# Split weight operands moved to 17 start offsets within larger buffers

## The chip, the cores and the metric

The kernel runs on one core of one Trainium2 chip. The metric is the device time of one execution in microseconds (us); the median of several runs is compared. The engines are called as in the profile: PE is TensorE's matmul stream, PEld its weight loads, DVE is VectorE, ACT is ScalarE, POOL is GpSimd, SP is SyncE, which here only issues DMAs.

## The reference, cut to what matters

One decoder layer over a sequence of 1024 rows of 1024 values, all in float32, and a last normalization:

```python
h = rms_norm(x, norm_mix)
proj = h @ w_in                       # 1024 x 8192, in eight groups of 1024 columns
xa, ga, q, f, v, g, m_a, m_b = split(proj)
y_a = rg_lru(conv(xa), w_r, w_i, ...) * gelu(ga)      # two 256-wide block products
y_b = rms_norm(hgrn2(silu(q), f, v)) * silu(g)
x = x + (sigmoid(m_a) * y_a + sigmoid(m_b) * y_b) @ w_out
h = rms_norm(x, norm_mlp)
x = x + square(relu(h @ w_up)) @ w_down               # 1024 x 4096, 4096 x 1024
return rms_norm(x, norm_final)
```

## The kernel before, in words

Every large product is made from three matmuls. `split` turns a float32 tile into a high part of type fp32r (ACT, line 76) and a low part, the difference (DVE, line 77). `mm3` (lines 113 to 117) adds high times low, high times high and low times high into one PSUM bank. In the trace a matmul reads `out<-moving,stationary`: `pj_f<-hT0H,wL` streams `hT0H` past the weights `wL`. The moving operand is 512 columns wide except in `project_v`, where it is 256.

The mixer takes the sequence in two halves (c = 0, 1) and each half in four pairs of heads (p = 0 to 3). For a pair, `project_v` makes v with the weights moving (out `pv`). `project` makes the other seven groups with the weights stationary and `hT`, the transposed input, moving (out `pj_xa`, `pj_q` and so on); `rg_lru` does its block products with the weights stationary and `xc` moving (out `pr`, `pi`). After four pairs `out_proj`, for c = 1 a loop of its own, multiplies by w_out with the weights moving (out `po`). The MLP works on 16 quads of hidden columns by a seven-product scheme: `hidden` streams `h2...` past split weights (out `uX`, `uY`, `uZ`), and the down products stream split weights past `u...` (out `dX`, `dY`, `dZ`), for two quads in turn, three matmuls for one quad and three for the other.

The numbered weight tiles are `wts[i]`, i from 0 to 75: 17 for a pair (v 0 and 1, xa 2 and 3, q 4 and 5, f 6 and 7, rg 8, then two each for g, mb, ga, ma), and eight of w_out. SP loads them into four buffers `raw`, and `split_w` (lines 87 to 92) splits each into `wH` and `wL`, which lie in six buffers under the tag `w`. The MLP's split tiles of 1024 columns lie in the same six buffers (line 771) for every quad up, and for one of the two quads of a down step. Buffers are taken as they come free; `split_w` has a raised priority, and its two instructions are kept in the order of the program up to the end of the first norm. A tile scheduler then orders the instructions of each engine by priority and writes the waits.

Byte addresses within a partition, as the allocator lays the buffers out: the six `w` buffers start at 23,296 and then every 4,096 bytes, `hT` fills 80,640 to 113,408, the split `xc` starts at 170,688, the `h2` tiles fill 114,624 to 229,312. In the down products the first quad's operands lie in the `w` buffers, in 47,872 to 56,064 and in 56,064 to 84,736, the second quad's at 131,008 to 163,776 (weights) and from 180,160 up (`u`). All of these starts are multiples of 64 bytes. Those of the `w` buffers, of `hT` and of the first quad are multiples of 256; those of `xc`, `h2` and of the second quad are 192 past a multiple of 256, so 64 past a multiple of 128. What a matmul reads starts at a multiple of 512 bytes within its tile.

Of the kernel before, what the change touches and what calls it, by code (L numbers as in the profile page):

```python
# [11 lines left out]
F32R = mybir.dt.float32r  # L12
# [6 lines left out]
P = 128  # L19
# [12 lines left out]
OUT_TILES = 8  # L32
QUADS = 16
LEVELS = (2, 8)


PV_LB, PV_CB, PV_BR, PV_BI, PV_LAM, PV_CW, PV_HG = 0, 8, 16, 24, 32, 40, 72
# [4 lines left out]
def trunk(ctx: ExitStack, tc: tile.TileContext, x, wts, mlp, pv, gains, mask_f, mask_u, out):  # L42
# [4 lines left out]
    wp = ctx.enter_context(tc.tile_pool(name="wp", bufs=1))  # L47
# [27 lines left out]
    def split(src, h, lo):  # L75
        keep(A.copy(h, src))  # L76
        keep(V.tensor_tensor(out=lo, in0=src, in1=h.bitcast(F32), op=ALU.subtract))  # L77
# [7 lines left out]
        return raw  # L85

    def split_w(i, raw):
        h = wp.tile([P, 1024], F32R, tag="w", name=f"wH{i}", bufs=6)
        lo = wp.tile([P, 1024], F32R, tag="w", name=f"wL{i}", bufs=6)
        with tc.high_priority(400):  # L90
            split(raw, h, lo)
        return h, lo
# [3 lines left out]
    def fill_w(n):  # L96
        while made[0] < min(n, len(seq)):
            i = seq[made[0]]
            raw = raws.pop(0) if raws else load_w(i)
            ready[made[0]] = split_w(i, raw)  # L100
            made[0] += 1
# [168 lines left out]
    def project(c, name):  # L270

        pp = [bank("pj", f"pj_{name}_{s}") for s in range(2)]
        for half in range(2):
            wh, wl = next_w()
            for k in range(4):
                hh, hl = kt(hT[c], 4 * half + k)
                for s in range(2):
                    cols = slice(k * 256 + s * P, k * 256 + (s + 1) * P)
                    mm3(pp[s], wh[:, cols], wl[:, cols], hh, hl, half == 0 and k == 0, half == 1 and k == 3)
        return pp  # L280
# [45 lines left out]
    def rg_lru(c, p, xc, xh, xl):  # L326
        wh, wl = next_w()
        hs = mt("h", f"h{c}{p}", (P, 2, T))
        for s in range(2):
            u = 2 * p + s  # L330
            pr, pi = bank("pj", f"pr{c}{u}"), bank("pj", f"pi{c}{u}")
            for o, k0 in ((pr, 0), (pi, 2)):
                for k in range(2):
                    cols = slice((k0 + k) * 256 + s * P, (k0 + k) * 256 + (s + 1) * P)
                    mm3(o, wh[:, cols], wl[:, cols], xh[:, k, :], xl[:, k, :], k == 0, k == 1)
            w = mt("rw", f"rw{c}{u}")
            A.activation(w, pr, AF.Sigmoid, bias=pvt[:, PV_BR + u : PV_BR + u + 1])
            A.activation(w, w, AF.Tanh, scale=sp4[:, u : u + 1])
            ig = mt("ri", f"ri{c}{u}")
            A.activation(ig, pi, AF.Sigmoid, bias=pvt[:, PV_BI + u : PV_BI + u + 1])  # L340

            V.tensor_scalar(w, w, 0.0, None, op0=ALU.max)
            rec = mt("rr", f"rr{c}{u}")
            V.tensor_scalar(rec, w, 1.0, None, op0=ALU.add)
            V.reciprocal(rec, rec)  # L345
            A.activation(w, w, AF.Sqrt)
            V.tensor_tensor(out=ig, in0=ig, in1=xc[:, s, :], op=ALU.mult)
            V.scalar_tensor_tensor(w, w, 2.0, rec, op0=ALU.mult, op1=ALU.mult)
            V.tensor_tensor(out=ig, in0=ig, in1=w, op=ALU.mult)
            V.tensor_scalar(rec, rec, 2.0, -1.0, op0=ALU.mult, op1=ALU.add)  # L350
            h = hs[:, s, :]
            V.tensor_tensor_scan(h, rec, ig, hcar[:, u : u + 1], op0=ALU.mult, op1=ALU.add)
            if c + 1 < NC:
                G.tensor_copy(hcar[:, u : u + 1], h[:, T - 1 : T])
        return hs
# [12 lines left out]
    def f_of(c, p, pp):  # L368
        ff = mt("f", f"f{c}{p}", (P, 2 * T))
        kk = mt("kk", f"kk{c}{p}", (P, 2 * T))  # L370
        for s in range(2):
            u = 2 * p + s
            f, k = ff[:, s * T : (s + 1) * T], kk[:, s * T : (s + 1) * T]
            A.activation(f, pp[s], AF.Sigmoid)
            A.activation(k, pp[s], AF.Sigmoid, scale=-1.0)
            V.tensor_scalar(f, f, omlb[:, u : u + 1], lb[:, u : u + 1], op0=ALU.mult, op1=ALU.add)
            V.tensor_scalar(k, k, omlb[:, u : u + 1], None, op0=ALU.mult)
        V.tensor_scalar(ff, ff, F_MIN, 1.0, op0=ALU.max, op1=ALU.min)
        return ff, kk

    def hgrn(c, p, q1, f, kk, v):
# [42 lines left out]

        for li, cw in enumerate(LEVELS):
            g = 256 // cw
# [199 lines left out]
    for c in range(NC):  # L626
# [6 lines left out]
        for p in range(NPAIR):  # L633
# [7 lines left out]
            f, kk = f_of(c, p, project(c, f"f{c}{p}"))  # L641
            with tc.high_priority(300):
                h = rg_lru(c, p, *xc3)
# [366 lines left out]
def _masks():  # L1010
# [3 lines left out]
    mu[:, 0, 0, :] = (t % 2 == 1) & (s == t - 1)  # L1014
    for i, c in enumerate(LEVELS):
        for d in (1, 2, 3):
# [32 lines left out]
```

## Time and profile before

| | before |
|---|---|
| median of 3 runs | 1634.1 us (1632.56 to 1635.3) |
| span of the profiled execution | 1630.3 us |
| PE busy | 1585.8 us, 97% |
| DVE busy | 1211.9 us, 74% |
| ACT busy | 762.2 us, 47% |
| PE matmuls, weight loads | 9240, 9240 |

The span runs from the first to the last instruction of the one execution that was profiled, and for that execution the page gives no other time; the median of the runs is 3.8 us above it. A record's duration of a matmul covers its whole way through the array, so consecutive records overlap. What a matmul costs in a dense stretch is read from the distance between the starts of consecutive ones.

### The profile page before, as it was taken

The numbers are of one execution on the slowest core, as the hardware profiler recorded it, in microseconds if no ns is written. First come the engines' busy times: TensorE is split into PE (matmuls) and PEld (weight loads), VectorE is DVE, ScalarE is ACT, GpSimd is POOL, SyncE is SP. The second block draws the span as 40 slices with busy tenths as digits, with TensorE's granted clock in tenths as the row PEclk, the third lists the DMA queues.
The fourth block names the chain that finished last, engine by engine and source line by source line (L and its number), as shares of the span: only waits on it lengthen the run. The fifth ranks groups of instructions, "written<-read, shape, count | busy, mean of one in ns | idle before, by whom it ended". The sixth has DMA issues, their size and how long they took to land.

```text
span 1630.3 us, 23190 instructions
## 1 busy us (share of the span) xinstructions
PE 1585.8 (97%) x9240; PEld 1303.6 (80%) x9240; DVE 1211.9 (74%) x1751; ACT 762.2 (47%) x1186; POOL 62.8 (4%) x99
## 2 busy tenths in 40 slices
PE   7999999999999999999999998999999999999998
PEld 6788788788788788788787876888888878888886
DVE  5975956848764965848759688977777888888876
ACT  4643545435442544436435566767766732221113
POOL 0010100100100000000100000000000000000000
PEclk9999999999999999999999998999999999999999
DMA  6222223223244222222222352666666566666652
GB/s 236 91 66 91 91 66 103 66 91 93 78 165 142 80 77 91 78 84 98 66 91 91 125 200 102 262 247 239 233 248 247 216 259 237 238 246 249 252 207 104
DMA packets 57996, 246.51 MB, mean 151 GB/s; under 512 B 6688, under 2 KB 6816, under 8 KB 47136
## 3 DMA queue, kind: packets, MB, share of 16 engines
q1 hardware_dynamic: 56304, 239.27, 40.8%
q10 hardware_dynamic: 1584, 5.77, 1.0%
q8 instruction: 72, 1.18, 0.3%
q14 instruction: 36, 0.29, 0.1%
HBM read 185.24 MB, written 59.77 MB: 150 GB/s over the span
## 4 chain that ended last, share of the span: by engine, by line
PE 82%; DVE 15%; issue 1%; ACT 1%; DMA 1%; POOL 0%; DVEq 0%; POOLq 0%; SPq 0%; ACTq 0%
PE dX L115 4%; PE dX L117 4%; PE dX L116 4%; PE uX L115 3%; PE uX L117 3%; PE uX L116 3%; DVE wL L77 2%; PE pj_ga L117 2%; PE pj_ga L116 2%; PE pj_ga L115 2%; PE pj_ma L117 2%; PE pv L116 2%; PE pv L115 2%; PE pj_ma L116 2%; PE pv L117 2%; PE pj_f L117 2%
## 5 line engine op out<-in xcount | busy, mean ns | idle before, releaser
L77 DVE TENSOR_TENSOR wL<-raw,wH 128x1024 fp32r<-128x1024 f32 x160 | 194.4, 1215 | 151.3 <-ACT wH L76 148.7
L76 ACT CAST wH<-raw 128x1024 fp32r<-128x1024 f32 x160 | 167.9, 1050 | 166.9 <-issue 67.1
L963 DVE TENSOR_TENSOR acc<-acc,dX 128x512 f32<-128x512 f32 x128 | 86.7, 682 | 29.6 <-PE dX L117 28.9
L76 ACT CAST wA<-q 128x512 fp32r<-128x512 f32 x32 | 19.8, 621 | 130.9 <-PE dX L117 82.8
L963 DVE TENSOR_TENSOR acc<-acc,dY 128x512 f32<-128x512 f32 x64 | 43.6, 683 | 16.6 <-PE dY L117 14.9
L345 DVE RECIPROCAL rr<-rr 128x512 f32<-128x512 f32 x16 | 53.5, 3345 | 0.0
L823 ACT ACTIVATE b<-b 128x512 f32<-128x512 f32 x48 | 30.2, 631 | 38.7 <-DVE b L822 38.6
L115 PE MATMUL pv<-wL,hT0H 128*128 128x256 f32 x128 | 37.1, 289 | 0.0
L117 PE MATMUL pv<-wH,hT0L 128*128 128x256 f32 x128 | 36.7, 286 | 0.0
L116 PE MATMUL pv<-wH,hT0H 128*128 128x256 f32 x128 | 36.6, 286 | 0.0
L115 PE MATMUL pv<-wL,hT1H 128*128 128x256 f32 x128 | 36.5, 285 | 0.0
L116 PE MATMUL pv<-wH,hT1H 128*128 128x256 f32 x128 | 36.2, 283 | 0.0
L117 PE MATMUL pv<-wH,hT1L 128*128 128x256 f32 x128 | 36.2, 283 | 0.0
L311 DVE SCALAR_TENSOR_TENSOR xc<-xp,pvt,xc 128x512 f32<-128x512 f32 x48 | 33.1, 746 | 0.0
L551 ACT ACTIVATE on<-po 128x128 f32<-128x128 f32 x64 | 17.0, 278 | 33.5 <-PE po L541 33.2
L570 ACT ACTIVATE smb<-pj_mb 128x512 f32<-128x512 f32 x16 | 9.6, 597 | 45.4 <-PE pj_mb L117 45.2
L824 ACT ACTIVATE b<-b 128x512 f32<-128x512 f32 x48 | 30.0, 629 | 1.1
L384 DVE TENSOR_TENSOR seg<-seg 128x128 f32<-128x128 f32 (+2 forms) x96 | 26.8, 309 | 0.2
L565 ACT ACTIVATE g<-pj_g 128x512 f32<-128x512 f32 x16 | 9.6, 598 | 37.2 <-PE pj_g L117 37.2
L444 POOL TENSOR_SCALAR seg<-seg 128x128 f32<-128x128 f32 (+1 forms) x16 | 12.6, 790 | 360.9 <-DVE seg L384 360.9
L117 PE MATMUL pj_ga<-hT1H,wL 128*128 128x512 f32 x64 | 26.5, 414 | 0.0
L115 PE MATMUL uX<-h2B11L,wA 128*128 128x512 f32 x64 | 26.2, 409 | 0.3 <-DVE rstd_h L137 0.3
(1854 smaller groups left out, 5258.3 us busy)
## 6 DMA issues: line engine op xcount, KB each, us to landing
raw<-wts_in SPq DMA_DIRECT2D x160, 512.0 KB, 3.5
q<-mlp_in SPq DMA_DIRECT2D x64, 512.0 KB, 4.0
x<-x_in SPq DMA_DIRECT2D x8, 512.0 KB, 5.6
acc<-x ACTq DMA_DIRECT2D x8, 512.0 KB, 6.0
y_out<-acc SPq DMA_DIRECT2D x16, 256.0 KB, 2.1
xs<-x_in SPq DMA_DIRECT2D x8, 256.0 KB, 4.2
x<-xs SPq DMA_DIRECT2D x8, 256.0 KB, 2.1
x2s<-x_in SPq DMA_DIRECT2D x4, 512.0 KB, 4.8
```

Source lines behind the costliest of these rows:

```text
L76: keep(A.copy(h, src))
L77: keep(V.tensor_tensor(out=lo, in0=src, in1=h.bitcast(F32), op=ALU.subtract))
L115: PE.matmul(o, ah, bl, start=first, stop=False, **how)
L116: PE.matmul(o, ah, bh, start=False, stop=False, **how)
L117: PE.matmul(o, al, bh, start=False, stop=last, **how)
L311: V.scalar_tensor_tensor(xc[:, s, :], xp[:, j : j + T], pvt[:, PV_CW + 8 * j + u : PV_CW + 8 * j + u + 1], xc[:, s, :], op0=ALU.mult, op1= ...
L345: V.reciprocal(rec, rec)
L384: mul = lambda o, a, b: V.tensor_tensor(out=o, in0=a, in1=b, op=ALU.mult)
L551: A.activation(on[:, 4 * s + n, :], po[:, n * P : (n + 1) * P], AF.Square, accum_out=ssq[:, 4 * s + n : 4 * s + n + 1])
L823: A.activation(b[:, at, :], b[:, at, :], AF.Relu, scale=-1.0 if at == 2 else 1.0)
L824: A.activation(b[:, at, :], b[:, at, :], AF.Square)
L963: V.tensor_tensor(out=dst, in0=dst, in1=banks[bk, pr], op=op)
```

## The change

A split weight tile no longer starts at the start of its buffer. The buffers of tag `w` grow from 1024 to 1072 elements of 4 bytes (4,288 bytes), and `wH` and `wL` of weight tile i are the 1024 elements that begin at element `START[i // 2 % 17]`: 0 to 48 elements, which is 0 to 192 bytes. High and low part of one tile have the same offset, and so have mostly the two tiles of a group.

```diff
+START = (0, 1, 2, 4, 6, 8, 10, 12, 14, 16, 24, 32, 36, 40, 44, 47, 48)
...
     def split_w(i, raw):
-        h = wp.tile([P, 1024], F32R, tag="w", name=f"wH{i}", bufs=6)
-        lo = wp.tile([P, 1024], F32R, tag="w", name=f"wL{i}", bufs=6)
+        at = START[i // 2 % len(START)]
+        h = wp.tile([P, 1072], F32R, tag="w", name=f"wH{i}", bufs=6)[:, at : at + 1024]
+        lo = wp.tile([P, 1072], F32R, tag="w", name=f"wL{i}", bufs=6)[:, at : at + 1024]
         with tc.high_priority(400):
             split(raw, h, lo)
```

The MLP's tiles under the same tag keep 1024 elements and start at the start of their buffer. But the buffers now stand 4,288 bytes apart, so every other one starts 64 past a multiple of 128. All that is allocated from the left behind them moves up by 6 x 192 = 1,152 bytes, which is nine times 128 and not a multiple of 256: `hT`, `xc` and the first quad's other tiles among them. What is allocated from the right (`h2`, the second quad's tiles) stays.

## The prediction

> **What bounds the kernel now.** I read the page first: busy times, slices, then the chain of work that ended last.
>
> ```profile
> PE 1585.8 (97%) x9240; PEld 1303.6 (80%) x9240; DVE 1211.9 (74%) x1751; ACT 762.2 (47%) x1186; POOL 62.8 (4%) x99
> ...
> PE   7999999999999999999999998999999999999998
> ...
> PEclk9999999999999999999999998999999999999999
> ...
> PE 82%; DVE 15%; issue 1%; ACT 1%; DMA 1%; POOL 0%; DVEq 0%; POOLq 0%; SPq 0%; ACTq 0%
> ```
>
> PE is busy in nearly every slice at the full granted clock, and the chain is PE for 82%. The table by stage says the same; its columns are the stretch in us, its length, then busy us of PE, PEld, DVE, ACT, POOL with instructions.
>
> ```profile
> 20.00:473.00 453.00, 446.08 (x3117) 373.26 (x3116) 322.02 (x503) 211.62 (x346) 31.87 (x47) 1.00 0.28 90
> ...
> 500.00:927.00 427.00, 421.46 (x2993) 351.92 (x2992) 295.06 (x437) 196.28 (x325) 20.78 (x28) 1.00 0.27 86
> ...
> 990.00:1314.00 324.00, 320.85 (x1369) 256.22 (x1367) 264.67 (x332) 224.01 (x320) 0.00 (x0) 1.00 0.60 228
> 1314.00:1620.00 306.00, 305.66 (x1319) 247.46 (x1320) 244.48 (x360) 65.02 (x92) 0.00 (x0) 1.00 0.58 224
> ```
>
> In the four dense stages, 1,510 us together, PE idles 16 us. So the change counts where it alters how fast matmuls follow each other. For that I read the timeline of PE: start in us, duration, line, operands. First and last row of five steady stretches:
>
> ```profile
> 127.56 0.28 PE L115 MATMUL pv<-wL,hT0H 128*128 128x256 f32 x1
> ...
> 137.88 0.28 PE L117 MATMUL pv<-wH,hT0L 128*128 128x256 f32 x1
> ```
>
> ```profile
> 62.64 0.39 PE L117 MATMUL pj_f<-hT0H,wL 128*128 128x512 f32 x1
> ...
> 74.88 0.39 PE L117 MATMUL pj_g<-hT0H,wL 128*128 128x512 f32 x1
> ```
>
> ```profile
> 55.00 0.39 PE L115 MATMUL pr<-xcL,wH 128*128 128x512 f32 x1
> ...
> 59.66 0.39 PE L117 MATMUL pi<-xcH,wL 128*128 128x512 f32 x1
> ```
>
> ```profile
> 1101.12 0.40 PE L116 MATMUL uZ<-h2B21H,wA125H 128*128 128x512 f32 x1
> ...
> 1109.05 0.40 PE L117 MATMUL uY<-h2B22H,ws35L 128*128 128x512 f32 x1
> ```
>
> ```profile
> 1404.82 0.39 PE L115 MATMUL dX<-wA1218L,u2t 128*128 128x512 f32 x1
> 1405.05 0.40 PE L116 MATMUL dX<-wA1218H,u2t 128*128 128x512 f32 x1
> 1405.28 0.40 PE L117 MATMUL dX<-wA1218H,u2t 128*128 128x512 f32 x1
> 1405.51 0.40 PE L115 MATMUL dX<-wA1219L,u3t 128*128 128x512 f32 x1
> 1405.75 0.39 PE L116 MATMUL dX<-wA1219H,u3t 128*128 128x512 f32 x1
> 1405.98 0.39 PE L117 MATMUL dX<-wA1219H,u3t 128*128 128x512 f32 x1
> 1406.21 0.39 PE L115 MATMUL dX<-wA1218L,u2t 128*128 128x512 f32 x1
> ```
>
> Starts per matmul: v, 256 columns, 10.32 us over 86 = 120.0 ns; projections 12.24 over 54 = 226.7; the block products of `rg_lru` 4.66 over 20 = 233; MLP up 7.93 over 34 = 233.2. The first two differ by 106.7 ns for 256 columns, so 512 columns stream in 213.3, and a matmul pays a fixed 13.3 ns; in the block products and MLP up it pays 20.0. The block products lie between two projections, in the same stage and with weights from the same six buffers: what differs is the moving operand. It starts at a multiple of 128 bytes in v and the projections, 64 past one in the other two. I call these moving operands on and off, and the price of off is **6.7 ns a matmul**. In the down products three matmuls with the first quad, on, take 0.69 us, and three with the second, off, 0.70: 233 each. The on ones lag behind 3 x 226.7 = 0.68, as if settling back takes some matmuls. The second quad's stationary operand is off too, and its 233 is no more than that of the block products, whose stationary is on.
>
> **The change part by part.**
>
> *What it does not add.* No instruction, byte or wait: the splits write and the matmuls read 1024 elements as before. The splits' cost I take as zero:
>
> ```profile
> L77 DVE TENSOR_TENSOR wL<-raw,wH 128x1024 fp32r<-128x1024 f32 x160 | 194.4, 1215 | 151.3 <-ACT wH L76 148.7
> L76 ACT CAST wH<-raw 128x1024 fp32r<-128x1024 f32 x160 | 167.9, 1050 | 166.9 <-issue 67.1
> ...
> L311 DVE SCALAR_TENSOR_TENSOR xc<-xp,pvt,xc x48: 742/746/753, 43.9 to 847.5; 128x512 f32<-128x512 f32 x48
> ...
> L302 ACT COPY xp<-pj_xa x16: 585/586/588, 40.1 to 843.6; 128x512 f32<-128x512 f32 x16
> ```
>
> The convolution reads `xp` on DVE at 0, 4 and 8 bytes past its start, and all 48 lie within 742 to 753 ns; ACT writes `xp` 12 bytes past it in 585 to 588, so start offsets of a few words show no spread. If each split took 1% longer, DVE would gain 2 us over the mixer, where it is idle for a quarter of the time; PE's idle 16 us bounds what is uncovered. Below zero: nothing waits there that would shrink.
>
> *Moving operands that become off.* Three groups, with the buffers now alternating between on and off starts.
> v: 4 pairs x 2 halves x 4 row tiles x 8 x 3 = 768 matmuls. The v tiles 17p and 17p+1 get offsets 0 and 0 (p = 0, 2) or 56 and 64 bytes (p = 1, 3). Offset 0 or 64 is off in half the buffers, 56 in all: 5/8, 480 matmuls, x 6.7 = 3.2 us.
> Output projection: 2 x 192 = 384 matmuls, offsets 0, 4, 8, 16 bytes, off in 7/8: 336 x 6.7 = 2.2.
> Down: 1,344, half with the first quad, six products of seven in the `w` buffers, half of these off: 288 x 6.7 = 1.9.
> Together **7.3 us**. Lower bound: only starts 64 past 128 count (288 of v, 192 of the output projection, 480 x 6.7 = 3.2), and a down triple loses 0.70 - 0.69, 96 x 0.01 = 1.0; that is 4.2. Upper bound by the settling seen above: where `wH` and `wL` lie in buffers of unlike start, the on ones don't settle either: 768 + 384 + 288 = 1,440 at 6.7 = 9.6.
> MLP up: moving `h2` stays off, so 0.
>
> *Stationary operands that become off.* The 2,688 projection matmuls and 192 block products get weights at all 17 offsets; 0 and 128 bytes keep the on buffers on, 64 and 192 the off ones, so 2 of 17, about 1/8, stay on: 2,520 become off. MLP up adds 1,344 x 6/7 x 1/2 = 576 at 64 bytes. The second quad's row prices 64 bytes at 0, and I take 0 for all. Upper bound: the moving price, 2,520 x 6.7 = 16.9 us. Below nothing: see the rivals.
>
> The Trainium skill, "TensorE: Matmul & The Clock Gate", section "Part 2: What happens when you issue a matmul", says PE has separate read ports for the moving operand and the weight load, so that loading doesn't take bandwidth from the running matmul. By that the stationary term is 0, as taken; without it the sum would be up to 24 us. The second quad's 0.70 us agrees.
>
> *The shift by 1,152 bytes.* `hT` goes from 0 to 128 past a multiple of 256. If the period of the effect is 128 it stays on: 0. If it is 256, 2,688 x 6.7 = 17.9 us. No row has a start at 128 in this type. I take 0, since the extra time of the off rows, 6.7 of 213.3 ns, is 1/32 of 2,048 bytes, so 64 bytes: the way from 64 to the next multiple of 128.
>
> *Offsets below 64 bytes as such.* Nearest rows, float32 matmuls of 48 columns:
>
> ```profile
> L394 PE MATMUL sc<-qb,kk 128*32 128x48 f32 x512 | 7.1, 207 | 5.0 <-DVE qb L384 5.0
> L394 PE MATMUL sc<-q,kk 128*32 128x48 f32 x512 | 7.1, 208 | 4.0 <-DVE q L384 4.0
> L394 PE MATMUL sc<-qa,kk 128*32 128x48 f32 x512 | 7.1, 208 | 0.9
> ```
>
> `qa` is read from column 2 of rows of 14, so at odd multiples of 8 bytes; `qb` and `q` at multiples of 32 or more. 207 to 208 ns, so 0. Odd words (offsets 4 and 188) are in no row; see the rivals.
>
> The Trainium skill, "SBUF — State Buffer", section "Door 1: The DMA port swizzle", says SBUF works in 16-byte lines, with a penalty for each crossing. By it only the six offsets that aren't multiples of 16 would cost, one line more in 128, and 64 would be free; the rows at 64 past 128, 6.7 ns dearer, differ, so the measurement decides. Its sum would be about 0.
>
> **Sum.** 0 + 7.3 + 0 + 0 + 0 = 7.3 us on the span of 1630.3, so 1637.6; the runs' median lies 3.8 above the span: **1641**, +0.45%. A change under 0.2%, 3.3 us, can't be told from none.
>
> **The rivals.**
> *It is the region, not the start.* Every 233 row streams from above byte 114,624, every 227 and 120 row from below 113,408; on and off coincide with that. Then nothing changes: 1634. Against it: 1/32 fits an address line better than a region.
> *Stationary starts or the 256 period count as well.* +16.9 or +17.9 on top: 1658 to 1659; both: 1676.
> *Faster: the fixed 13.3 ns is a clash of weight load and moving read that both start at multiples of 256.* Offset weights would avoid it. Place: 2,520 projections and block products; price up to 13.3 ns, 33 us less; with 7.3 against it 1608. It decides from 7.3/2,520 = 2.9 ns a matmul. For it: all 226.7 rows have both on. Against: with the moving operand 64 bytes away from the stationary, the gap is longer, not shorter.
> *Odd words are read at half rate.* Offsets 4 and 188 fall on tiles 2, 3, 30, 31, 36, 37, 64, 65 (xa and ga, 384 loads) and 70, 71 (96 moving matmuls).
>
> ```profile
> L117 PEld LDWEIGHTS pj_xa<-hT0H,wL x64: 187/188/188, 29.9 to 363.5; 128*128 128x128 f32 x64
> ```
>
> A load of 188 ns doubled would stand 149 over the 226.7 it hides under: 57 us, plus 96 x 213 = 20: up to 1718.
>
> **How the numbers follow.** Moving starts alone (1638 to 1644): 0.34. Stationary or period too (1650 to 1676): 0.24. Region, nothing changes: 0.22. Faster: 0.10. Odd words: 0.10. Slower 0.34 + 0.24 + 0.10 less 0.03 for small sums = 0.65; same 0.22; faster 0.13, with 0.03 from small shifts of the schedule. The range 1629 to 1664 holds nearly all of the first and third, most of the second and a little of the others, about 0.8. The likeliest case alone: 1638 to 1644.
>
> **What would show it.** Projections at 226.7 ns still, whatever the weights' offset (stationary 0, period 128); 233 or more would hand it to the second rival, under 224 to the faster one. v at 126.7 where the moving start is off; 120.0 throughout means region. Output projection at 233. Block products and MLP up unchanged. A weight load over 200 ns in xa of pair 0 means odd words. Wrong would be the price if it grew with the offset, or the settling if it cost more than 6.7.

## The result and the profile after

The change makes the kernel slightly slower. The median went from 1633.3 us (20 runs) to 1636.56 us (20 runs, 1634.59 to 1638.94), ratio 1.0019 [1.0013, 1.0026]. The sign was forecast, but not the size: 1641, 0.45%. The profiled execution took 1636.08 us, with a span of 1634.3, 4.0 above the span of before.

The page of after, busy times and the granted clock by slices:

```profile
PE 1594.4 (98%) x9240; PEld 1303.9 (80%) x9240; DVE 1211.8 (74%) x1751; ACT 760.8 (47%) x1186; POOL 62.7 (4%) x99
...
PEclk9999999999999999999999998999999999999999
```

Nothing new runs and the clock is the same, but PE is busy 8.6 us longer in a span that grew by 4.0. The table by stage shows both. Its stretches go from the first `pv` to the first `u`, on to the first `dX`, and on to the last matmul. Columns as in the prediction, the second number being the length. First before, then after:

```profile
11.30:988.90 977.60, 954.13 (x6538) 796.20 (x6537) 693.27 (x1044) 465.35 (x761) 59.99 (x86) 1.00 0.31 101
988.90:1305.60 316.70, 314.64 (x1341) 251.81 (x1342) 256.66 (x321) 218.00 (x311) 0.55 (x1) 0.99 0.59 226
1305.60:1622.30 316.70, 314.81 (x1357) 253.96 (x1355) 254.44 (x373) 73.37 (x107) 0.00 (x0) 1.00 0.58 226
```

```profile
11.20:996.50 985.30, 967.04 (x6538) 796.59 (x6537) 694.11 (x1044) 464.59 (x761) 59.83 (x86) 1.00 0.30 100
996.50:1309.40 312.90, 310.97 (x1341) 251.78 (x1342) 255.47 (x321) 217.33 (x311) 0.55 (x1) 0.99 0.60 229
1309.40:1626.20 316.80, 314.18 (x1356) 253.96 (x1355) 254.70 (x373) 73.39 (x107) 0.00 (x0) 1.00 0.59 226
```

Two large terms of opposite sign nearly cancel. The mixer grew by 7.7 us, MLP up shrank by 3.8, down stayed. In the mixer PE's busy time grew by 12.9 and its idle time (length less busy) fell from 23.5 to 18.3, so 5.2 us of the dearer matmuls were absorbed by waits. Most of that is one wait, the 48-column matmuls `sc` on DVE's `q`. Waits of PE before, then after (us in total, times, longest):

```profile
PE xT_x L145 <- DVE xn L139: 11.0, 2, 9.5
...
PE sc L394 <- DVE qb L384: 5.0, 8, 0.6
PE sc L394 <- DVE q L384: 4.0, 8, 0.5
```

```profile
PE xT_x L147 <- DVE xn L141: 10.3, 2, 9.4
...
PE sc L396 <- DVE qb L386: 4.7, 8, 0.6
...
PE sc L396 <- DVE q L386: 0.5, 3, 0.2
```

The timeline of PE in after, the first and last row of each stretch. The first three stretches are a projection, the block products and MLP up; then come two down triples, the w_out tiles at byte 4, and v in pair 1:

```profile
62.61 0.39 PE L119 MATMUL pj_f<-hT0H,wL 128*128 128x512 f32 x1
...
75.13 0.39 PE L119 MATMUL pj_g<-hT0H,wL 128*128 128x512 f32 x1
```

```profile
55.00 0.40 PE L117 MATMUL pr<-xcL,wH 128*128 128x512 f32 x1
...
59.61 0.39 PE L119 MATMUL pi<-xcH,wL 128*128 128x512 f32 x1
```

```profile
1108.22 0.39 PE L118 MATMUL uZ<-h2B21H,wA125H 128*128 128x512 f32 x1
...
1115.33 0.40 PE L119 MATMUL uY<-h2B22H,ws35L 128*128 128x512 f32 x1
```

```profile
1408.43 0.40 PE L117 MATMUL dX<-wA1218L,u2t 128*128 128x512 f32 x1
...
1409.13 0.39 PE L117 MATMUL dX<-wA1219L,u3t 128*128 128x512 f32 x1
...
1409.81 0.39 PE L117 MATMUL dX<-wA1218L,u2t 128*128 128x512 f32 x1
```

```profile
462.84 0.40 PE L117 MATMUL po<-wL,y0H 128*128 128x512 f32 x1
...
471.36 0.40 PE L117 MATMUL po<-wL,y0H 128*128 128x512 f32 x1
```

```profile
127.65 0.28 PE L117 MATMUL pv<-wL,hT0H 128*128 128x256 f32 x1
...
137.87 0.28 PE L119 MATMUL pv<-wH,hT0L 128*128 128x256 f32 x1
```

Projection: 12.52 us over 54 matmuls, 231.9 ns (before 226.7). Block products: 4.61 over 20, 230.5 (233). MLP up: 7.11 over 31, 229.4 (233.2). Down: 0.70 and 0.68 for three (0.69 and 0.70). Output projection: 8.52 over 36, 236.7. v: 10.22 over 86, 118.8 (120.0). For whole groups I take the mean distance between starts of consecutive matmuls of one shape, leaving out the gaps in which PE waited. In ns, with four kernels of the experiments below:

| group (matmuls) | before | after | pitch_only | pitch_128 | offsets_only | right_256 |
|---|---|---|---|---|---|---|
| projections (2,688) | 227.5 | 231.9 | 231.8 | 232.2 | 231.8 | 227.5 |
| block products (192) | 233 | 232 | 231 | 231 | 233 | 233 |
| output projection (384) | 227.3 | 233.6 | 231.5 | 230.6 | 232.4 | 227.3 |
| v, 256 columns (768) | 119.9 | 118.8 | 118.3 | 117.9 | 119.4 | 119.95 |
| MLP up (1,344) | 233.3 | 230 | 230 | 232 | 233.3 | 227 |
| down (1,344) | 232 | 231 | 231 | 231 | 232 | 227 |

Before to after, by matmuls: projections 2,688 x 4.4 = +11.8 us, output projection +2.4, block products -0.2, v -0.85, MLP up -4.4, down -0.8. That is +7.9, PE's busy time (+8.6) within 0.7 us.

### The profile page after: what moved, and what is told of

It reads as the page before. It is cut to its first block, busy times and chain, and to the rows that moved or that the text cites. A ratio compares the mean times of both kernels' runs of the same rounds, so it can differ in the third digit from the quotient of the medians.

```text
span 1634.3 us, 23190 instructions
## 1 busy us (share of the span) xinstructions
PE 1594.4 (98%) x9240; PEld 1303.9 (80%) x9240; DVE 1211.8 (74%) x1751; ACT 760.8 (47%) x1186; POOL 62.7 (4%) x99
## 4 chain that ended last, share of the span: by engine, by line
PE 82%; DVE 14%; DMA 1%; issue 1%; ACT 1%; POOL 0%; DVEq 0%; POOLq 0%; SPq 0%
PE dX L117 3%; PE dX L118 3%; PE dX L119 3%; PE uX L117 3%; PE uX L119 3%; PE uX L118 3%; DVE wL L78 2%; PE pj_ga L119 2%; PE pj_q L117 2%; PE pj_ma L119 2%; PE pj_xa L117 2%; PE pj_ga L117 2%; PE pj_xa L119 2%; PE pj_ga L118 2%; PE pj_ma L117 2%; PE pj_q L118 2%
## 5 line engine op out<-in xcount | busy, mean ns | idle before, releaser
L78 DVE TENSOR_TENSOR wL<-raw,wH 128x1024 fp32r<-128x1024 f32 x160 | 194.6, 1216 | 154.3 <-ACT wH L77 151.5
L77 ACT CAST wH<-raw 128x1024 fp32r<-128x1024 f32 x160 | 167.5, 1047 | 174.2 <-issue 67.8
L386 DVE TENSOR_TENSOR kk<-kk,seg 128x768 f32<-128x768 f32 (+1 forms) x32 | 26.2, 819 | 0.3 <-DVE dd L440 0.3
```

The lines of the kernel that those rows point to most:

```text
L386: mul = lambda o, a, b: V.tensor_tensor(out=o, in0=a, in1=b, op=ALU.mult)
```

## The experiments

I first held two theories against each other. *Like starts*: a matmul costs 226.7 ns when its two operands start alike modulo 256, and more otherwise. The prediction's *moving alone* is the other; *region* stood beside them. Times of the layer are medians of 4 to 12 executions, against before on the same chip; each kernel of matmuls alone ran once, at a granted clock of 1.0.

### streams: matmuls alone, 38 combinations of starts

A kernel with only the matmul loop, everything loaded beforehand, 144 matmuls in the order of `mm3` for each combination (`ml`, `mh`, `sh`, `sl`: start bytes past a multiple of 256 of moving low and high, stationary high and low):

```diff
+TRIPLES = 48
...
+    for name, ml, mh, sh, sl, cols, reg in CASES:
...
+        for t in range(TRIPLES):
...
+            for j, (a, b) in enumerate(((h, lo), (h, hi), (l, hi))):
+                PE.matmul(o, sta[:, a : a + P], m[:, b : b + cols], start=j == 0, stop=j == 2)
```

> Leaves the layer out: only matmuls of type fp32r, in 38 stretches of 144 with nothing else running, each stretch with its own starts (bytes past a multiple of 256) of the moving low and high operand and of the stationary high and low one; the output is not the layer's. The prediction's theory, moving start alone, period 128: 226.7 ns a matmul wherever both moving starts are 0 or 128 (aa, ac, ae, af, ag, aj, ak, al, ap, ar, at, av, ba, bc, bd, bf), 233.3 where they are 64 or 192 (ab, ad, ah, ai, be), between these or 233.3 for small starts. Rival, like starts: what counts is whether the reads of consecutive matmuls and weight loads start alike; then ah, ai, aw, ax, ay also run at 226.7, ae, ag, aj, ak, am, an at 230 to 234. Rival, region: aa to bc all at 226.7, bd, be, bf (moving operand above byte 126,208) at 233.3. 256 columns: 120.0 in bg, 126.7 in bh by the first theory.

Rows of the named outputs; the last columns are the first and the last start of the 144 in us, so their difference over 143 is the spacing. `ai`: both operands at 192. `ad`: moving 192, stationary 0. `au`: moving 4. `aw`: both 4. `bg` and `bh`: 256 columns, moving 0 and 64, stationary 0.

```profile
L66 PE MATMUL ai<-x,w x144: 388/389/393, 279.1 to 311.5; 128*128 128x512 f32 x144
L66 PE MATMUL ad<-x,w x144: 390/394/394, 112.8 to 146.2; 128*128 128x512 f32 x144
L66 PE MATMUL au<-x,w x144: 393/398/401, 679.5 to 713.4; 128*128 128x512 f32 x144
L66 PE MATMUL aw<-x,w x144: 397/400/401, 747.1 to 781.1; 128*128 128x512 f32 x144
L66 PE MATMUL bg<-x,w x144: 274/283/283, 1081.0 to 1098.2; 128*128 128x256 f32 x144
L66 PE MATMUL bh<-x,w x144: 279/279/282, 1098.3 to 1115.1; 128*128 128x256 f32 x144
```

In the steady part (last 96) `ai` runs at 226.7 ns, as with both at 0, at 32 or at 64; `ad` 233.3, `au` 236.7, `aw` 237.8, both at 16 230.0. *Like starts* had expected 226.7 for these last two as well, so alike alone is not enough. With the moving operand at 0 and the stationary at 64, 128, 192: 233.3, 232.4, 228.9; with the stationary at 0 and the moving at 64, 128, 192: 228.9, 232.4, 233.3. So the stationary start counts as much as the moving one, which ends *moving alone*; and 192 is cheap if both have it, which ends a price per start. At 256 columns the order is reversed: 120.0 with both at 0, 117.8 with either operand at 64; but moving at 4 costs 123.3.

### streams2: the difference alone, and region

The same kernel with moving starts in steps of 16 and the start pairs of after's MLP up.

```diff
-    ("ab", 64, 64, 0, 0, 512, 0), ...
+    ("tab", 16, 16, 0, 0, 512, 0), ... ("taq", 128, 128, 64, 64, 512, 0), ("tar", 128, 128, 0, 0, 512, 0), ...
```

> Leaves out the whole layer: 38 stretches of 144 fp32r matmuls in the order of `mm3` and nothing else, each stretch with its own start bytes of moving and stationary operand past a multiple of 256. Theory 'like starts' (what counts is the distance of the moving from the stationary start, modulo 256): 226.7 ns at distance 0; about 229 at 64, 232.4 at 128, 233.3 at 192; 229 to 234 at every other multiple of 16; with the moving operand at 128, stationary at 64, 0 and 192 gives 229, 232.4 and 233.3, as for the same distances from 0; the eight pairs with the moving operand at 192 and unlike high and low weights lie between 227 and 234 and average about 230; 256 columns 120.0 at distance 0 and about 118 at all others. Rival 'each operand by its own start' (a price for each start away from a multiple of 256, added up): moving at 128 with stationary at 64, 0 and 192 costs 232.4 or more throughout, and none of the eight pairs is under 233. Rival 'the tile's place counts beside the start': the tile at the upper end of the memory repeats 233.3 with the stationary operand at 192 where the lower one repeats 228.9, and differs at 64 too.

Moving at 128; stationary at 64, 0 and 192:

```profile
L91 PE MATMUL taq<-x,w x144: 388/392/398, 548.3 to 581.1; 128*128 128x512 f32 x144
L91 PE MATMUL tar<-x,w x144: 388/393/405, 581.3 to 614.5; 128*128 128x512 f32 x144
L91 PE MATMUL tas<-x,w x144: 391/396/399, 614.7 to 648.1; 128*128 128x512 f32 x144
```

Steady: 228.9, 232.3, 233.3, as for distances 64, 128, 192 from 0. So for these starts the distance decides, and not the place. Of the other steps of 16 all gave 231.1 to 234.7, except 240, where 226.7 came too, against the theory. The same distance with moving at 0 and stationary at 16 had cost 233.3 in `streams`, so the distance is not the whole rule. The eight pairs of MLP up gave 228.9 to 234.2, mean 231.6, where about 230 was expected and MLP up in after takes 230: the stretches give half of its gain. At 256 columns moving at 32, 64 and 192 took 117.8 and at 128 118.7, but at 56 120.0, where about 118 was expected. A tile at the upper end of the memory gave the same 226.7 (0 and 0) and 228.9 (stationary 192) as the lower one: region is out. In `streams` the upper tile had 233.3 for that second pair; streams3 shows below that one pair can have both.

### pitch_only and pitch_128: larger buffers, no offsets

The pitch is the distance from the start of one `w` buffer to the next. pitch_only changes one line of after:

```diff
-        at = START[i // 2 % len(START)]
+        at = 0
```

and for pitch_128 besides (the same for `lo`)

```diff
-        h = wp.tile([P, 1072], F32R, tag="w", name=f"wH{i}", bufs=6)[:, at : at + 1024]
+        h = wp.tile([P, 1056], F32R, tag="w", name=f"wH{i}", bufs=6)[:, at : at + 1024]
```

> All 17 offsets are 0, the buffers stay 4,288 bytes apart and what follows stays moved by 1,152 bytes. If the unlike buffer starts (every other one 64 past a multiple of 128) and the shift of hT to 128 past a multiple of 256 make the loss: the whole of the change's +3 us, projections at 231 to 232 ns as after it. If the 17 offsets make it: 1633, projections at 226.7. The prediction's theory: v and w_out off in half the buffers, down as predicted, 768/2 x 6.7 + 384/2 x 6.7 + 1.9 = +5.8 us, projections at 226.7.

> Offsets 0, buffers 4,224 bytes apart (33 x 128), so their starts alternate between 0 and 128 past a multiple of 256, and what follows moves by 768 bytes, hT stays at a multiple of 256. Period 128: nothing changes, 1633, projections at 226.7, MLP up at 233.3. Period 256: projections at 231 to 232 and up to +12 us in the mixer.

Pitch 4,288 alone: 1635.24 us against 1633.9, ratio 1.0011 [1.0002, 1.002]; its twelve runs spread from 1633.1 to 1639.6. That is less than the whole +3 us that was expected, though the interval overlaps that of after. Pitch 4,224: 1638.79, 1.003 [1.0018, 1.0041]. The pitch alone makes the projections as dear as in after (231.8), and MLP up as cheap (230): the offsets add next to nothing to either. Pitch 4,224 shows that 128 is not the period. There `hT` moves by 6 x 128 = 768, three times 256, and every second buffer starts 128 past a multiple of 256, yet the projections cost 232.2.

### offsets_only: the 17 offsets, every buffer where it was modulo 256

Of after, this line, the same for `lo`, and 512 instead of 1,024 bytes of DMA scratch at the start of the memory:

```diff
-        h = wp.tile([P, 1072], F32R, tag="w", name=f"wH{i}", bufs=6)[:, at : at + 1024]
+        h = wp.tile([P, 1088], F32R, tag="w", name=f"wH{i}", bufs=6)[:, at : at + 1024]
```

> The changed kernel with buffers of 1088 instead of 1072 elements (pitch 4,352 bytes, 17 x 256), and 512 bytes instead of 1,024 of scratch, so that every buffer and everything behind it stands as in the kernel before, modulo 256. Only the 17 offsets act. Like starts: projections about 232 ns where they were 227.5 (+12 us over 2,688), output projection about 232 (+1.8 us), v 118.8 (-0.8 us); MLP up 233.3 and down 231.5 as before, so the changed kernel's gain in MLP up (4 us) is absent; with 4 to 5 us taken up by PE's waits on DVE, 1641 to 1643. Rival 'the pitch does it, the offsets are idle': projections 227.5, the time of the kernel before, 1633. Rival of the prediction (moving starts alone): projections 226.7 to 227.5, +2 to +5 us from v and the output projection, 1635 to 1638.

1642.74 us against 1633.61, ratio 1.0058 [1.0045, 1.0071], in the range expected. By stage:

```profile
11.20:996.10 984.90, 966.71 (x6538) 797.66 (x6536) 694.05 (x1044) 464.71 (x761) 59.82 (x86) 1.00 0.29 100
996.10:1312.80 316.70, 314.89 (x1341) 252.55 (x1342) 256.72 (x322) 217.97 (x311) 0.55 (x1) 0.99 0.59 226
1312.80:1632.60 319.80, 315.65 (x1356) 254.01 (x1355) 254.55 (x373) 73.39 (x107) 0.00 (x0) 1.00 0.58 223
```

The mixer costs 7.3 more than before, MLP up is as before to 0.1 us. So after's gain in MLP up comes from the pitch, its loss in the mixer from either. The two parts don't add up (+1.3 and +9.1 give +3.3), in part since two ways of starting unlike cost the projections no more than one (the mixer grew by 5.8 with the pitch alone, 7.3 here, 7.7 in after), in part by 3.1 us in down that after doesn't have. Those 3.1 us, at the spacing of before, come with longer waits of `dX` on DVE and are not explained. Without them the time would lie below the expected range, so that hit is partly luck.

### right_256: the cheap direction

In the kernel before, 48 words more of padding at the right end, so that `h2` and the second quad's tiles too start at a multiple of 256:

```diff
-    pad.tile([P, 8], F32, tag="pad", name="pad")
+    pad.tile([P, 56], F32, tag="pad", name="pad")
```

> The kernel before with 192 bytes more of padding at the right end, so that h2 and the second quad's tiles start at multiples of 256 instead of 192 past one; the w buffers, hT and xc as before. Starts count (moving alone or like starts): MLP up at 226.7 instead of 233.3, 1,344 x 6.7 = 9.0 us less, down at 226.7 instead of 232.2, 1,344 x 5.5 = 7.4 less: 1617. Region: 1633, all as before.

1622.11 us against 1633.9, ratio 0.9929 [0.9917, 0.9941]; run again in a later comparison, as the partner of v_64, 1622.44, 0.9927 [0.9913, 0.994].

> The kernel before with 192 bytes more padding, unchanged, as the partner of the run above on one chip: 1622, ratio 0.993, v at 119.95 ns by all theories.

Stages of the first profile, and the waits in it that before does not have:

```profile
988.30:1299.90 311.60, 307.88 (x1341) 251.00 (x1342) 255.49 (x322) 216.76 (x311) 0.55 (x1) 0.99 0.59 230
1299.90:1615.70 315.80, 309.97 (x1356) 253.45 (x1355) 253.57 (x373) 73.52 (x107) 0.00 (x0) 1.00 0.58 226
```

```profile
PE dX L115 <- DMA u10n<-u10n: 1.5, 1, 1.5
...
PE dX L115 <- DMA u4n<-u4n: 1.1, 1, 1.1
```

All of MLP up and down now run near 227 ns: 1,344 x 6.3 and 1,344 x 5 or so, 15 us by spacing, of which 11.8 reach the median: 1622, not the 1617 expected. In this execution, the slowest of its five (1625.33 us), PE is busy 4.8 us less in down and gives most of that back (stage 316.7 to 315.8), with 3.7 us of waits for the transfer of the second quad's `u`. In the second profile these waits are 1.0 us and the stage takes 313.4. After (0.7) and pitch_128 (1.5) have such waits too, without faster down products, so it isn't shown that the speed of the products brings them on.

### all_256 and all_256_order: the rest of it

Both keep right_256's padding. all_256 also widens `xp` to 576 and `mf` to 64 columns, so that `xc` starts at a multiple of 256; all_256_order also changes the order of the four transfers of `load_u`:

```diff
-        for g in U_GROUPS:
+        for g in (U_GROUPS[0], U_GROUPS[3], U_GROUPS[1], U_GROUPS[2]):
```

> The kernel before with 192 bytes more padding at the right end (as in the run before, 0.9929) and `xp` and `mf` widened to multiples of 256 bytes, so that `xc` starts at a multiple of 256 as well: every matmul of 512 columns then has like starts. Like starts: the 192 block products fall from 233 to 226.7 ns, 1.2 us, so 1621, ratio 0.992. Rival 'the block products pay for something else': no change against 1622.

> The kernel above, with the DMAs of the second quad's `u` (the four groups of `load_u`) issued in the order 0, 3, 1, 2. In the run with 192 bytes of padding the down products ran 7.4 us faster by their spacing, but the stage only 1 us, with waits of PE on the transfers of `u..n`. If it is the order of arrival that holds them: those waits go, up to 4 us less, 1617 to 1620. Rival 'the queue's amount binds, not its order': another group is late instead, 1621 as without it.

1621.18 us, 0.9924 [0.9911, 0.9936], and 1622.29, 0.9928 [0.9915, 0.9942]. The block products fell to 227 to 229 ns as expected, a gain of 1 us that two runs' medians can't tell. The new order removed no time. In its profile PE waits 4.6 us on the `t` group:

```profile
PE dY L115 <- DMA u8t<-u8t: 1.3, 1, 1.3
PE dY L115 <- DMA u6t<-u6t: 1.3, 1, 1.3
...
PE dY L115 <- DMA u10t<-u10t: 1.1, 1, 1.1
```

all_256, the same kernel with the old order, has 0.4 us of waits for `u` in its profile:

```profile
PE dX L115 <- DMA u10n<-u10n: 0.4, 1, 0.4
```

So the new order doesn't help, and its waits are not those of right_256 moved elsewhere; whether the queue's amount binds was not tried.

### v_64: unlike starts where they help

right_256, with v's weight tiles alone 64 bytes up in buffers of pitch 4,352 (and the DMA scratch at 512 bytes, as in offsets_only):

```diff
+        at = 16 if i < 68 and i % 17 < 2 else 0
```

> The kernel with 192 bytes more padding, and in it the weight tiles of v alone (i % 17 under 2) moved 64 bytes up, in buffers of 1088 elements (pitch 4,352 bytes, 17 x 256, so nothing else changes its start modulo 256; scratch 512 bytes). Like starts, with the 256-column rows of the stretches (120.0 ns at distance 0, 117.8 at 64): v falls from 119.95 to about 117.8 ns, 768 x 2.1 = 1.6 us; all other products stay at 226.7 to 227.5; some of it may go to waits, so 0.5 to 1.6 us below the run beside it without the move. Rival 'a price for every start away from 256': v rises to 121 or more.

1620.88 us, 0.9919 [0.9905, 0.9932], the lowest median of all, though not told apart from right_256 (0.9927). In the profile v's mean falls from 119.95 to 116.4 ns, below the 117.8 expected, and the mixer from 977.1 and 976.9 (right_256's two profiles) to 974.4, which is 768 x 3.6 = 2.7 us:

```profile
11.30:985.70 974.40, 951.97 (x6538) 793.99 (x6537) 693.59 (x1044) 466.18 (x761) 60.10 (x86) 1.00 0.29 101
```

At 256 columns starts 64 apart pay, as in `bh`; the rival, a price for every start away from 256, is refuted here as well.

### streams3: whose starts must agree

One row of the layer contradicts like starts: in the kernel before both operands of every down product start alike (0 and 0, or 192 and 192, three by three), and still cost 232. The same loop with a cycle of pairs (moving, stationary):

```diff
+    ("uab", ((0, 0), (64, 64)), 512),
+    ("uac", ((0, 64), (64, 0)), 512),
...
+    ("uah", ((0, 0), (0, 0), (0, 0), (192, 192), (192, 192), (192, 192)), 512),
...
+    ("uau", ((0, 192),), 512),
+    ("uav", ((192, 0),), 512),
+    ("uaw", ((0, 192),), 512),
```

> Leaves out the whole layer: 23 stretches of 144 fp32r matmuls, each with a cycle of start bytes (moving, stationary) past a multiple of 256. Open after the other runs: in the kernel before, the down products alternate between a quad with both operands at 0 and one with both at 192, alike in each matmul, and still cost 231 to 232 ns. Theory 'the next load' (what counts is the moving operand that streams against the stationary operand that is being loaded at that time, which is the next matmul's): cycles whose matmuls are alike but change the start each time (0/0, 64/64; 0/0, 128/128; 0/0, 192/192; the cycle of four) cost 229 to 234; cycles with unlike matmuls in which each stationary start equals the moving start of the matmul before (0/64, 64/0; 0/128, 128/0; 0/192, 192/0; four: 0/192, 64/0, 128/64, 192/128) cost 226.7; three at 0/0 and three at 192/192, the down products of before, 228 to 232, and 226.7 when the first stationary of each three is given the start of the moving operand before it; 256 columns 120.0 at 0/0 and at 0/64, 64/0, about 118 at 0/0, 64/64. Rival 'own pair' (a matmul's two operands alike or not): the alike cycles 226.7 throughout, the crossed ones 229 to 234, and the down products of before then pay for something else, such as the change of tiles.

```profile
L73 PE MATMUL uab<-x,w x144: 388/393/398, 48.1 to 81.3; 128*128 128x512 f32 x144
...
L73 PE MATMUL uac<-x,w x144: 388/393/397, 81.5 to 114.6; 128*128 128x512 f32 x144
...
L73 PE MATMUL uah<-x,w x144: 387/394/401, 247.8 to 281.0; 128*128 128x512 f32 x144
...
L73 PE MATMUL uau<-x,w x144: 388/392/394, 631.0 to 663.7; 128*128 128x512 f32 x144
...
L73 PE MATMUL uaw<-x,w x144: 392/397/398, 697.5 to 730.9; 128*128 128x512 f32 x144
```

Both theories fail at 512 columns. Steady, `uab` (each pair alike) takes 231.7 and `uac` (each stationary start that of the moving one before it) 231.7. `uah`, the down products of before, takes 232.2, their 232, and even the gaps repeat: 226, 236, 232, 240, 226, 234 ns, in before 226, 236, 231, 240, 227, 233. Of the changing starts none reached 226.7. The cheapest took 228.3, among them 0 and 0, then 128 and 128 in turn; with 12 pairs at 0 and 12 at 192 in turn it was 228.9, and there about ten matmuls are dearer after one change and three after the other. So every 226.7 but one (moving at 240) came with both operands at the same 0, 32, 64 or 192 *and* the same start from matmul to matmul. At 256 columns what 'the next load' expected did come: 120.0 for 0/0 and for 0/64, 64/0, and 116.7 for 0/0, 64/64; this was not followed up. `uau` and `uaw` have the same starts, yet steady spacings of 228.9 and 233.3; `uau` follows a stretch at 0 and 0, `uaw` one at 192 and 0. So what went before decides too, which a sum of prices per start can't hold. Why the two streams hold each other up is not shown by any run.

## Why the prediction was wrong, point by point

That the kernel got slower as forecast was luck. The +7.3 us were all moving terms, and these came to +0.8 (output projection +2.4, v -0.85, down -0.8). The loss came from the projections, put at 0, and MLP up and shorter waits, put at 0 too, took most of it back.

**The price, 6.7 ns for a moving start off the 128 grid.** Its size was right (226.7 to 233.3 recurs in the stretches), its cause wrong. Block products and MLP up were dear because `xc` and `h2` at 192 met weights at 0, not because 192 is a dear place: `ai` streams from 192 at 226.7. This reading, one operand of two, gave all later terms.

**Stationary operands, 0 (projections).** This is the step that failed. It came out at 2,688 x 4.4 = 11.8 us, within its upper bound of 16.9. It was read from the second quad's triple, 0.70 us at a stationary start of 192. But that triple's moving start was 192 too and changed every three matmuls, so the row held two effects and could not price the stationary one. (Nor were the two triples 233 each: 0.69 and 0.70 us for three are 231 and 233 ns each in the trace.) The prediction took the row to agree with the Trainium skill's separate read ports ("TensorE: Matmul & The Clock Gate", "Part 2: What happens when you issue a matmul"). The runs don't agree that loading is therefore free: with the moving operand at 0, the spacing is 226.7 or 233.3 by the start of the weights alone.

**Period 128, so the shift by 1,152 costs 0.** Wrong: 128 against 0 costs 232.4, and pitch_128 shows it in the layer. It cost nothing on top, since the projections were unlike already.

**Moving terms: v +3.2, output projection +2.2, down +1.9.** v came out at -0.85, since at 256 columns unlike is the cheap case; no row of before with 256 columns had unlike starts, and a gain should have been its lower bound. The output projection came to +2.4, near enough, but by starts as such and by the odd words of two tiles (236.7). Down came to -0.8. The lower bound had a slip as well: of the output projection's offsets 0, 4, 8 and 16 only 0 gives starts 64 past 128, so 48 matmuls instead of 192, and a bound of about 3.2 us instead of 4.2.

**MLP up, 0.** It came out at -4.4: the new pitch brought the `w` buffers to four starts modulo 256, and some of those suit `h2` at 192 better than 0 did (streams2: 228.9 to 234.2 instead of 233.3). "Moving `h2` stays off" looked at one operand of two. The sum had no term that could be negative outside the rivals.

**From matmuls to span, one for one.** Another failed step. 7.9 us by matmuls became 4.0 of span, 5.2 of the mixer's 12.9 going into waits that got shorter. The wait of `sc` on `q` follows the projections in every profile: 4.0 us where they take 227.5 ns (before, right_256, v_64), 0.4 to 1.3 where they take 232 (after, both pitches, offsets_only). The prediction had its chain at PE 82%, DVE 15%, and did not ask what that 15% does when PE slows.

**Splits 0, no added work.** Right: DVE's split takes 1,216 ns after 1,215, ACT's 1,047 after 1,050.

**The rivals.** The second, stationary starts and period, had the mechanism in the projections but priced it without the gains elsewhere. Region is out (streams2). Odd words at half rate: no weight load of `pj_xa` or `pj_ga` is over 194 ns, and byte 4 costs 10 ns of the stream, not 213. The faster one guessed that two reads at multiples of 256 clash: the opposite of what 512 columns show, and the direction that 256 columns show (120.0 to 117.8).

## What to carry to other kernels

Start the moving and the stationary operands of all dense float32r streams of 512 columns at the same place modulo 256 (0, 32, 64 and 192 were cheap, 4 and 16 were not, others weren't tried), and keep that place across the tiles of a loop: 192 bytes of padding gave 0.9929 here. For 256 columns the cheap case is another, so measure each width. Before a row prices an effect, list what else differs in it, the other operand and the matmul before included; and where PE slows down evenly, take off its waits on engines that keep their pace.

## What the runs showed of the hardware

In the kernels of matmuls alone, for 512 columns and weights loaded for each matmul, the spacing lay between 226.7 and 237.8 ns by start addresses alone, at the full clock; for 256 columns between 116.7 (starts alike but changing between 0 and 64) and 123.3 (moving at 4). The dearest were starts at 4 (236.7 moving, 237.8 both). The Trainium skill's 16-byte lines ("SBUF — State Buffer", "Door 1: The DMA port swizzle") would put a price on every start that is no multiple of 16 and on no other. Moving at 4, 8 and 188 does cost more than at 0 (236.7, 233.3, 230.0). But multiples of 16 cost too: moving at 192 takes 233.3, more than at 188, so the measurement decides. The same pair of starts has two steady spacings, 228.9 and 233.3, depending on the stretch before.
